# Ring slots staggered by 32 bytes, and matrix inputs placed at another offset for each pass

## The chip, the cores and the metric

The kernel runs on one core of one Trainium2 chip. The metric is device time in microseconds (us): the median of the runs. An execution has a span, from its first to its last recorded instruction, and a time that is a little longer.

## The reference, cut to what matters

Two transformer blocks of two layers each follow one another on 256 tokens of width 1024, all in float32. The first block mixes (latent attention, a short convolution, stick-breaking attention) and then sends each token to 16 of 16,384 experts in each of 8 heads. The second block has windowed attention with 256 context tokens, a Fourier mix, and a gated feed-forward pass of width 2816, for the latent tokens and, in its first layer, for the context too.

```
def token_block(args):                        # experts of the first block
    u = jnp.take(u_tab, eb, axis=0)
    act = jax.nn.gelu(jnp.einsum('tkd,td->tk', u, hb), approximate=False)
    vv = jnp.take(v_tab, eb, axis=0)
    return jnp.einsum('tk,tkd->td', gb * act, vv)
...
def swiglu(h, w_gate, w_up, w_down):          # feed-forward of the second block
    return (jax.nn.silu(h @ w_gate) * (h @ w_up)) @ w_down
```

## The kernel before, in words

Nothing is gathered for the experts: all 16,384 are computed for all 256 tokens, and a matrix of gates that is mostly zero is multiplied in between the two products. So each expert layer is two large dense products, with the tables U (up) and V (down) streamed once.

**A product in three parts.** A float32 product runs as three fast matmuls of the type fp32r: high times high, high times low, low times high (mm3, L293 to L296). A weight tile of 128 x 1024 comes by DMA into a slot of the ring raw (5 slots, issued by SP); for each half of 512 columns ACT writes the rounded high part wh (L261) and DVE the rest wl (L263). Helper wtile (L271) does this; wh and wl have 5 slots each. TensorE's reading sets a slot free for ACT.

**Two roles of the ring.** A matmul has a stationary operand of 128 x 128, loaded by LDWEIGHTS while the matmul ahead still runs, and a moving operand whose columns are then streamed.
- On the up side (gemm_t, L298) wh and wl are stationary, and the input (hh and hl, f or mix) is moving, 256 columns long. Groups pact (U), pwq (expert queries), pwg and pwu (gate and up), pw (input projection), and sq, sk, cb, cc, ch.
- On the down side wh and wl are moving, 512 columns long, and the activations are stationary: acc (V, with WHL), and po (with a and b, the feed-forward activations, or with mix). In both down sides the four outputs of a tile are taken in turn over tokens tb and halves n, three matmuls each, so that the moving slot changes every three matmuls. kw is a kept copy of such weights.

**Where the operands lie.** The addresses below are those in the built program, in bytes of a partition, modulo 256. "Distance" is the moving operand's address less the stationary one's, modulo 256, from -127 to 128. In the kernel before a slot is 2048 bytes long, so all slots of wh and wl lie at 192. hh, hl and f lie at 224 on the up side; WHL, a and b at 192 on the down side (pool tiles of SHIFT = 56 floats more give this); mixT and the second block's pw input at 224. Of the 15,624 split matmuls, 11,184 have 256 columns (10,608 at distance +32, 480 at +64, 96 at -64), 96 have 416 columns (-64), and 4344 have 512 columns (4104 at 0, 240 at -32; those are the first po stages on mix). The scores of the second block's attention, psc, are fp32r matmuls too, of 256 columns at distance 0; like the other small products of attention they are not in these counts.

**Order.** Each engine runs a list written out by the program; the tile scheduler orders it, and the sizes and offsets of tiles enter only through which tile shares memory with which.

Of the kernel before, what the change touches and what calls it, by code (L numbers as in the profile page):

```python
# [25 lines left out]
F32 = mybir.dt.float32  # L26
F32R = mybir.dt.float32r
# [9 lines left out]
S, D, L = 256, 1024, 2  # L37
KB = D // 128
# [3 lines left out]
FB = 22  # L42
# [163 lines left out]
def kernel(ctx: ExitStack, tc: tile.TileContext, a: dict, out: bass.AP):  # L206
    nc = tc.nc
    V, SC, T, G, SP = nc.vector, nc.scalar, nc.tensor, nc.gpsimd, nc.sync
# [3 lines left out]
    ring = ctx.enter_context(tc.tile_pool(name="ring", bufs=3))  # L212
    dram = ctx.enter_context(tc.tile_pool(name="dram", bufs=1, space=DRAM))
    RAW, NHL = 5, 5
# [39 lines left out]
    def raw_tile(src, shape):  # L254
        r = ring.tile([128] + shape, F32, name="raw", tag="raw", bufs=RAW)
        SP.dma_start(r, src)
        return r

    def split(dst_h, dst_l, src):
        with after(PIN.get("act")):  # L260
            SC.activation(dst_h, src, AF.Copy)  # L261
        with after(PIN.get("dve")):
            return V.tensor_tensor(dst_l, src, dst_h, op=OP.subtract).ins  # L263

    LAST = [None]
    PIN = {}

# [3 lines left out]
    def wtile(src, shape, cuts=None, keep=None):  # L271


        r = raw_tile(src, shape)
        parts = []
        c0 = 0
        for cut in cuts or [shape[0] // 2] * 2:
            sh = [cut] + shape[1:]
            h, lo = [(keep or ring).tile([128] + sh, F32R, name=nm, tag=nm, bufs=4 if keep else NHL) for nm in ("wh", "wl")]
            LAST[0] = split(h, lo, r[:, c0:c0 + cut])  # L280
            parts.append((h, lo))
            c0 += cut
        return parts
# [2 lines left out]

    SHIFT = 56

    def shifted(p, nm):
        t = p.tile([128, SHIFT + 2 * FB * S + 8], F32R, name=nm)[:, SHIFT:SHIFT + 2 * FB * S]  # L290
        return [t[:, i * FB * S:(i + 1) * FB * S].rearrange("p (f t) -> p f t", f=FB) for i in range(2)]

    def mm3(o, lh, ll, rh, rl, first, last):  # L293
# [518 lines left out]
    def peer(l, nxt):  # L812
# [2 lines left out]
        st.enter_context(banks(f"pa{l}", a=4, g=3))  # L815
        stpa = ExitStack()
        pa = stpa.enter_context(pool(f"peer{l}", side="right"))
        hh = pa.tile([128, KB, S], F32R, name="hh", tag="ha")
        hl = pa.tile([128, 2048 + SHIFT + 8], F32R, name="hl", tag="hb")[:, :2048].rearrange("p (k t) -> p k t", k=KB)
        idxT = pa.tile([128, 4, S], F32, name="idxT", tag="c")  # L820
        hot = pa.tile([128, 1 + 3 * NHOT, 128], F16, name="hot", tag="d")
        iota16 = hot[:, 0]
# [2 lines left out]
        with pool(f"topk{l}") as p:  # L825
            sh, sc = mod_cols(1, l, 3), mod_cols(1, l, 4)
# [16 lines left out]
            s = [p.tile([128, 16, 128], F32, name=f"s{tb}") for tb in range(2)]  # L843
# [160 lines left out]
        n = (128 - j) // 2  # L1004
# [6 lines left out]
        stb = ExitStack()  # L1011
        stb.enter_context(banks(f"pb{l}", acc=2, m=3))
        acc = [bank([128, 2, 512], f"acc{tb}", "acc") for tb in range(2)]
        Ws = pa.tile([128, 4, 2, S], F32, name="Ws", tag="ha")
        WHL = pa.tile([128, 2048 + SHIFT + 8], F32R, name="WHL", tag="hb")[:, SHIFT:SHIFT + 2048]
        WHL = WHL.rearrange("p (a b c t) -> p a b c t", a=2, b=2, c=2)
        stl, stk = ExitStack(), ExitStack()
        held = {}
# [6 lines left out]
        order = [120, 122, 124, 126] + list(range(0, 120, 2))  # L1025
# [45 lines left out]
        lgb = stl.enter_context(pool(f"lgb{l}", side="right")).tile([128, 2, D], F32, name="lgb")  # L1071
        for i in range(2):
            SP.dma_start(lgb[:, i], bcast_row(a["rows1"][l, 2 + i], D))
        rl = pa.tile([128, 2, D], F32, name="rl2", tag="ha")
        for tb in range(2):
            if l:
                next(nxt)
# [28 lines left out]
    def second_layer(l, p0, xc, c2, cosT, sinT, sm2, sink, pre):  # L1106
        both = l == 0
# [7 lines left out]
        def proj_out(p, s, src, nkt, mh, ml, gpart, row, tags=("mix", "gpr", "jk"), keep=None, jkp=None, mid=None,  # L1115
                     last=False):


            ssq = [p0.tile([128, 2], F32, name=f"sq{tb}", bufs=2) for tb in range(2)]
            gpr = p.tile([128, 2, D], F32, name="gpr", tag=tags[1])  # L1120
            gr, pr = gpr[:, 0], gpr[:, 1]
            SP.dma_start(pr, bcast_row(row, D))
            mod_row(gr, 2, l, gpart, s)
            V.tensor_tensor(gr, gr, pr, op=OP.mult)
            ps = [[bank([128, 512], "po", "m") for tb in range(2)] for n in range(2)]

            def mul(n, kt, tb, w):
                t = slice(128 * tb, 128 * tb + 128)
                for c in range(2):
                    k = 2 * kt + c  # L1130
                    mm3(ps[n][tb], mh[:, k, t], ml[:, k, t], w[c][0][:, 0], w[c][1][:, 0], k == 0, k == 2 * nkt - 1)

            def gated(n, tb):
                V.tensor_tensor(mixs[:, tb, n], ps[n][tb], gr[:, 512 * n:512 * n + 512], op=OP.mult)

            def square(n, tb):
                jk = (jkp or p).tile([128, 512], F32, name="jk", tag=tags[2], bufs=1)
                SC.activation(jk, ps[n][tb], AF.Square, accum_out=ssq[tb][:, n:n + 1])
                if n == 0:
                    gated(n, tb)  # L1140

            def tail(tb):
                ss = p0.tile([128, 1], F32, name="ss", bufs=2)
                V.tensor_tensor(ss, ssq[tb][:, 0:1], ssq[tb][:, 1:2], op=OP.add)
                r = rms_from(ss, D)
                gated(1, tb)
                x = xs[s][:, tb]
                if last:
                    for n in range(2):
                        c = slice(512 * n, 512 * n + 512)  # L1150
                        V.scalar_tensor_tensor(x[:, c], mixs[:, tb, n], r, x[:, c], op0=OP.mult, op1=OP.add)
                        SP.dma_start(out[0, 128 * tb:128 * tb + 128, c], x[:, c])
                else:
                    V.scalar_tensor_tensor(x, flat(mixs[:, tb]), r, x, op0=OP.mult, op1=OP.add)

            mixs = p.tile([128, 2, 2, 512], F32, name="mix", tag=tags[0])
            for n in range(2):
                ws = []
                for kt in range(nkt):
                    if keep and n:  # L1160
                        w = keep.tile([128, 2, 2, 512], F32R, name=f"kw{kt}")
                        r = raw_tile(src[n, kt], [2, 512])
                        for c in range(2):
                            split(w[:, c, 0], w[:, c, 1], r[:, c])
                        ws.append([(w[:, c, 0:1], w[:, c, 1:2]) for c in range(2)])
                        continue
                    w = wtile(src[n, kt], [2, 512])
                    if n and kt >= nkt - 2:
                        ws.append(w)
                    else:  # L1170
                        for tb in range(2):
                            mul(n, kt, tb, w)
                    if mid and (n, kt) == mid[0]:
                        mid[1]()
                for tb in range(2):
                    for kt, w in enumerate(ws, nkt - len(ws)):
                        mul(n, kt, tb, w)
                    square(n, tb)
                    if n:
                        tail(tb)  # L1180
# [250 lines left out]
        H, act, fp = {}, {}, {}  # L1431
# [4 lines left out]
        early = []  # L1436

        def tops(s, hp, px, ne=0):
            H[s] = [hp.tile([128, KB, S], F32R, name=f"f{i}{s}", tag=f"f{i}") for i in range(2)]
            cs = cols(l, s, 3, 8, "f")  # L1440
            for tb in range(2):
                hf = make_hT(px[tb], xs[s][:, tb], "rms", cs[0], cs[1], *H[s], 128 * tb, "m", px.count(px[tb]) if px[tb] is not fx else 1)
                for i in range(ne):
                    if tb == 0:
                        early.append((raw_tile((a["wg"], a["wu"])[i % 2][l, i // 2], [KB, 128]), bank([128, S], "pg", "m")))
                    gemm_early(early[i][1], early[i][0], hf, 128 * tb)
# [16 lines left out]


        fa1 = stp.enter_context(pool(f"ffa{l}"))
        act[order[0]] = shifted(fa1, "a")
        if both:
            fh0 = stp.enter_context(pool(f"ffg{l}"))
            sta = ExitStack()
# [3 lines left out]
        for s in order:  # L1473
            if both and s == 0:
                ex.run()
                stv.close()
                fa0 = sta.enter_context(pool(f"ffb{l}", side="right"))
                act[0] = shifted(fa0, "b")
            for f in range(FB):
                if s:  # L1480
                    ex.run(18.0 / (FB - 2))
                pgu = [e[1] for e in early[2 * f:2 * f + 2]] if s == 0 else []
                for nm in ("wg", "wu")[len(pgu):]:
                    pgu.append(bank([128, S], "p" + nm, "m"))
                    gemm_t(pgu[-1], wtile(a[nm][l, f], [KB, 128]), *H[s], 0, S)
                pg, pu = pgu
                sg = fx.tile([128, S], F32, name="sg", bufs=2)
                SC.activation(sg, pg, AF.Silu)
                V.tensor_tensor(sg, sg, pu, op=OP.mult)
                split(act[s][0][:, f], act[s][1][:, f], sg)  # L1490
                if s and f == FB - 6:
                    tops(0, fh0, [fx, fx])
# [46 lines left out]
```

## Time and profile before

| | us |
|---|---|
| median of 3 runs (lowest, highest) | 2849.2 (2847.5, 2852.63) |
| profiled execution: time, span | 2851.75, 2849.8 |
| TensorE matmul (PE) busy, share of the span | 2783.1, 98% |
| weight load (PEld) | 2437.5, 86% |
| VectorE (DVE) | 2197.0, 77% |
| ScalarE (ACT) | 1672.4, 59% |

The profiled execution lies inside the range of the runs. A matmul's record overlaps the next one's, since matmuls are pipelined; how long one occupies TensorE is read as the time from its start to the next one's start, and over a row of them as the difference of two starts divided by the intervals between. Mean durations of groups (280 to 390 ns) are not that time.

### The profile page before, as it was taken

How to read it: one execution, taken by the hardware profiler on the slowest of the kernel's cores; microseconds unless marked ns; L12 is line 12 of the kernel's file. 1: busy time of each engine (PE TensorE's matmuls, PEld its weight loads, DVE VectorE, ACT ScalarE, POOL GpSimd, SP SyncE). 2: the span in 40 equal slices, each digit the busy share in tenths (PEclk: the TensorE clock that was granted, in tenths of full speed). 3: DMA queues.
4: the chain of work that ended last, by engine and by line, in shares of the span. 5: the costliest groups of instructions: out<-in, count | busy, mean ns of one | idle time of the engine just before them, and what ended most of it. 6: DMA issues, size and time to landing. Idle time of an engine off the chain costs nothing.

```text
span 2849.8 us, 53010 instructions
## 1 busy us (share of the span) xinstructions
PE 2783.1 (98%) x19114; PEld 2437.5 (86%) x19114; DVE 2197.0 (77%) x5110; ACT 1672.4 (59%) x3459; POOL 39.2 (1%) x50
## 2 busy tenths in 40 slices
PE   7989999999999999999999999999999999998999
PEld 4569999998887766899999888878769999887997
DVE  4459999887789767799899777898769766577565
ACT  3435558885555445555799655555546555566554
POOL 0000000000000000000000000000000000000000
PEclk9999999999999999999999999999999999999999
DMA  9785775667789866576666777977647665652455
GB/s 325 234 275 180 241 233 193 200 202 253 240 275 310 302 240 236 200 236 230 208 198 198 238 240 241 335 270 221 225 157 268 215 204 189 205 184 70 159 187 162
DMA packets 188114, 639.76 MB, mean 224 GB/s; under 512 B 22709, under 2 KB 24117, under 8 KB 187209
## 3 DMA queue, kind: packets, MB, share of 16 engines
q1 hardware_dynamic: 179208, 604.90, 64.4%
q10 hardware_dynamic: 8640, 31.46, 2.8%
q8 instruction: 150, 2.46, 0.3%
q14 instruction: 116, 0.94, 0.1%
HBM read 600.06 MB, written 34.64 MB: 223 GB/s over the span
## 4 chain that ended last, share of the span: by engine, by line
PE 90%; DVE 4%; DMA 3%; ACT 2%; issue 1%; POOL 0%; SPq 0%; DVEq 0%; POOLq 0%; ACTq 0%
PE pact L294 9%; PE pact L296 8%; PE pact L295 8%; PE acc L295 8%; PE acc L296 8%; PE acc L294 8%; PE po L294 3%; PE po L295 3%; PE po L296 3%; PE adap L348 2%; DMA adaw<-in_ada_dram 2%; PE pwu L296 2%; PE pwu L294 2%; PE pwu L295 2%; PE pwg L294 2%; PE pwg L296 2%
## 5 line engine op out<-in xcount | busy, mean ns | idle before, releaser
L261 ACT ACTIVATE wh<-raw 128x512 fp32r<-128x512 f32 (+1 forms) x1636 | 1008.4, 627 | 809.0 <-PE acc L296 272.8
L263 DVE TENSOR_TENSOR wl<-raw,wh 128x512 fp32r<-128x512 f32 (+1 forms) x1636 | 1089.8, 683 | 378.1 <-ACT wh L261 372.8
L294 PE MATMUL pact<-hh,wh 128*128 128x256 f32 x2048 | 583.6, 285 | 0.0
L296 PE MATMUL pact<-hh,wl 128*128 128x256 f32 x2048 | 572.5, 280 | 0.2 <-DVE wl L263 0.2
L295 PE MATMUL pact<-hl,wh 128*128 128x256 f32 x2048 | 571.4, 279 | 0.0
L295 PE MATMUL acc<-wl,WHL 128*128 128x512 f32 x1024 | 399.3, 390 | 1.6 <-DVE wl L263 1.6
L294 PE MATMUL acc<-wh,WHL 128*128 128x512 f32 x1024 | 397.9, 390 | 1.2 <-ACT WHL L261 1.2
L296 PE MATMUL acc<-wh,WHL 128*128 128x512 f32 x1024 | 398.7, 389 | 0.0
L295 PEld LDWEIGHTS pact<-hl,wh 128*128 128x128 f32 x2048 | 385.5, 188 | 0.0
L294 PEld LDWEIGHTS pact<-hh,wh 128*128 128x128 f32 x2048 | 385.3, 188 | 0.0
L296 PEld LDWEIGHTS pact<-hh,wl 128*128 128x128 f32 x2048 | 384.9, 188 | 0.4 <-DVE wl L263 0.4
L295 PEld LDWEIGHTS acc<-wl,WHL 128*128 128x128 f32 x1024 | 192.2, 188 | 44.2 <-DVE wl L263 3.8
L294 PEld LDWEIGHTS acc<-wh,WHL 128*128 128x128 f32 x1024 | 192.2, 188 | 43.9 <-ACT WHL L261 3.3
L296 PEld LDWEIGHTS acc<-wh,WHL 128*128 128x128 f32 x1024 | 192.2, 188 | 40.4 <-DVE WHL L263 0.9
L993 ACT ACTIVATE hot<-hot,idxT 128x128 f16<-128x128 f16 x512 | 174.0, 402 | 1.3 <-DVE hot L992 1.2
L992 DVE TENSOR_SCALAR hot<-hot,idxT 128x128 f16<-128x128 f16 x512 | 158.0, 309 | 20.1 <-PE pG L994 19.8
L296 PE MATMUL pwu<-f,wl 128*128 128x256 f32 x512 | 143.1, 279 | 1.6 <-DVE wl L263 1.6
L294 PE MATMUL pwg<-f,wh 128*128 128x256 f32 x512 | 143.1, 280 | 0.0
L296 PE MATMUL pwg<-f,wl 128*128 128x256 f32 x512 | 143.0, 279 | 0.0
L295 PE MATMUL pwg<-f,wh 128*128 128x256 f32 x512 | 142.9, 279 | 0.0
L294 PE MATMUL pwu<-f,wh 128*128 128x256 f32 x512 | 142.8, 279 | 0.0
L295 PE MATMUL pwu<-f,wh 128*128 128x256 f32 x512 | 142.8, 279 | 0.0
(475 smaller groups left out, 5075.4 us busy)
## 6 DMA issues: line engine op xcount, KB each, us to landing
raw<-in_U_dram SPq DMA_DIRECT2D x256, 512.0 KB, 3.6
raw<-in_V_dram SPq DMA_DIRECT2D x256, 512.0 KB, 4.2
adaw<-in_ada_dram SPq DMA_DIRECT2D x192, 512.0 KB, 6.1
raw<-in_wg_dram SPq DMA_DIRECT2D x66, 512.0 KB, 4.2
raw<-in_wu_dram SPq DMA_DIRECT2D x66, 512.0 KB, 3.4
raw<-in_wd_dram SPq DMA_DIRECT2D x66, 512.0 KB, 4.2
spill<-gab ACTq DMA_DIRECT2D x60, 512.0 KB, 5.1
Ws<-spill SPq DMA_DIRECT2D x120, 256.0 KB, 3.8
```

Source lines behind the costliest of these rows:

```text
L261: SC.activation(dst_h, src, AF.Copy)
L263: return V.tensor_tensor(dst_l, src, dst_h, op=OP.subtract).ins
L294: T.matmul(o, lh, rh, start=first, stop=False)
L295: T.matmul(o, lh, rl, start=False, stop=False)
L296: T.matmul(o, ll, rh, start=False, stop=last)
L348: T.matmul(ps[32 * q:32 * q + 32, :], cvec(blk, k), r[h][:, 512 * (q % 2):512 * (q % 2) + 512], start=k == 0, stop=k == KB - 1, skip_group ...
L992: V.tensor_scalar(B, iota16, i2, g, op0=OP.is_equal, op1=OP.mult)
L993: SC.activation(B2, B, AF.Copy, scale=share)
```

## The change

The ring's wh and wl tiles become 516 floats wide, of which 512 are used, so that slots lie 2080 bytes apart, 32 bytes on from one to the next modulo 256. A first dummy load of 128 x 672 into raw and a gap tile of 24 floats, which is set to zero once, set the order and place of the ring's tags. The inputs are put at other offsets by placed and shifted. The pools' tiles grow by 64 floats to allow it, and the kernel's entry takes a smaller scratch area for DMA descriptors. No matmul is added, dropped or reshaped.

| operand, modulo 256 | before | after |
|---|---|---|
| wh and wl, slots 1 to 5 | 192 each | 192, 224, 0, 32, 64 |
| hh, hl of the mixer's projection; catH, wok | 0; 0, 0 | 160; 160, 160 |
| hh, hl of the experts, layer 0 / 1 | 224 / 224 | 224 / 48 |
| WHL, layer 0 / 1 | 192 / 192 | 192 / 112 |
| f: context; latent layer 0; latent layer 1 | 224 each | 128; 112; 176 |
| a; b | 192; 192 | 192; 208 |
| mixT and the first layer's pw input; kw | 224; 224 | 128; 224 |

Distances of the split matmuls after the change, in counts:

| distance | -112 | -96 | -80 | -64 | -48 | -32 | -16 | 0 |
|---|---|---|---|---|---|---|---|---|
| 256 columns | 408 | 1164 | 408 | 1128 | 192 | 816 | 876 | 720 |
| 512 columns | 312 | 72 | 306 | 48 | 306 | 0 | 54 | 594 |

| distance | 16 | 32 | 48 | 64 | 80 | 96 | 112 | 128 |
|---|---|---|---|---|---|---|---|---|
| 256 columns | 684 | 744 | 888 | 336 | 876 | 444 | 1068 | 432 |
| 512 columns | 54 | 414 | 54 | 468 | 360 | 498 | 354 | 450 |

```diff
--- before.py
+++ after.py
@@ -262,6 +262,17 @@
         with after(PIN.get("dve")):
             return V.tensor_tensor(dst_l, src, dst_h, op=OP.subtract).ins
 
+
+    def part_tile(p, sh, nm, bufs):
+        n = math.prod(sh)
+        t = p.tile([128, 516], F32R, name=nm, tag=nm, bufs=bufs)[:, :n] if p is ring else p.tile([128, n], F32R, name=nm, tag=nm, bufs=bufs)
+        return t if len(sh) == 1 else t.rearrange("p (a b) -> p a b", a=sh[0])
+
+    raw_tile(a["w1n"][0, 0:128, :], [672])
+    part_tile(ring, [4], "wh", NHL)
+    V.memset(ring.tile([128, 24], F32, name="gap", bufs=1), 0.0)
+    part_tile(ring, [4], "wl", NHL)
+
     LAST = [None]
     PIN = {}
 
@@ -276,7 +287,7 @@
         c0 = 0
         for cut in cuts or [shape[0] // 2] * 2:
             sh = [cut] + shape[1:]
-            h, lo = [(keep or ring).tile([128] + sh, F32R, name=nm, tag=nm, bufs=4 if keep else NHL) for nm in ("wh", "wl")]
+            h, lo = [part_tile(keep or ring, sh, nm, 4 if keep else NHL) for nm in ("wh", "wl")]
             LAST[0] = split(h, lo, r[:, c0:c0 + cut])
             parts.append((h, lo))
             c0 += cut
@@ -286,8 +297,12 @@
 
     SHIFT = 56
 
-    def shifted(p, nm):
-        t = p.tile([128, SHIFT + 2 * FB * S + 8], F32R, name=nm)[:, SHIFT:SHIFT + 2 * FB * S]
+    def placed(p, nm, tag, at):
+
+        return p.tile([128, 2048 + 64], F32R, name=nm, tag=tag)[:, at:at + 2048].rearrange("p (k t) -> p k t", k=KB)
+
+    def shifted(p, nm, at):
+        t = p.tile([128, 2 * FB * S + 64], F32R, name=nm)[:, at:at + 2 * FB * S]
         return [t[:, i * FB * S:(i + 1) * FB * S].rearrange("p (f t) -> p f t", f=FB) for i in range(2)]
 
     def mm3(o, lh, ll, rh, rl, first, last):
@@ -815,8 +830,7 @@
         st.enter_context(banks(f"pa{l}", a=4, g=3))
         stpa = ExitStack()
         pa = stpa.enter_context(pool(f"peer{l}", side="right"))
-        hh = pa.tile([128, KB, S], F32R, name="hh", tag="ha")
-        hl = pa.tile([128, 2048 + SHIFT + 8], F32R, name="hl", tag="hb")[:, :2048].rearrange("p (k t) -> p k t", k=KB)
+        hh, hl = [placed(pa, nm, tag, 20 * l) for nm, tag in (("hh", "ha"), ("hl", "hb"))]
         idxT = pa.tile([128, 4, S], F32, name="idxT", tag="c")
         hot = pa.tile([128, 1 + 3 * NHOT, 128], F16, name="hot", tag="d")
         iota16 = hot[:, 0]
@@ -1011,8 +1025,8 @@
         stb = ExitStack()
         stb.enter_context(banks(f"pb{l}", acc=2, m=3))
         acc = [bank([128, 2, 512], f"acc{tb}", "acc") for tb in range(2)]
-        Ws = pa.tile([128, 4, 2, S], F32, name="Ws", tag="ha")
-        WHL = pa.tile([128, 2048 + SHIFT + 8], F32R, name="WHL", tag="hb")[:, SHIFT:SHIFT + 2048]
+        Ws = pa.tile([128, 2048 + 64], F32, name="Ws", tag="ha")[:, :2048].rearrange("p (a b t) -> p a b t", a=4, b=2)
+        WHL = placed(pa, "WHL", "hb", SHIFT - 20 * l).rearrange("p k t -> p (k t)")
         WHL = WHL.rearrange("p (a b c t) -> p a b c t", a=2, b=2, c=2)
         stl, stk = ExitStack(), ExitStack()
         held = {}
@@ -1071,7 +1085,7 @@
         lgb = stl.enter_context(pool(f"lgb{l}", side="right")).tile([128, 2, D], F32, name="lgb")
         for i in range(2):
             SP.dma_start(lgb[:, i], bcast_row(a["rows1"][l, 2 + i], D))
-        rl = pa.tile([128, 2, D], F32, name="rl2", tag="ha")
+        rl = pa.tile([128, 2048 + 64], F32, name="rl2", tag="ha")[:, :2048].rearrange("p (a d) -> p a d", a=2)
         for tb in range(2):
             if l:
                 next(nxt)
@@ -1117,7 +1131,7 @@
 
 
             ssq = [p0.tile([128, 2], F32, name=f"sq{tb}", bufs=2) for tb in range(2)]
-            gpr = p.tile([128, 2, D], F32, name="gpr", tag=tags[1])
+            gpr = p.tile([128, 2048 + 64], F32, name="gpr", tag=tags[1])[:, :2048].rearrange("p (a d) -> p a d", a=2)
             gr, pr = gpr[:, 0], gpr[:, 1]
             SP.dma_start(pr, bcast_row(row, D))
             mod_row(gr, 2, l, gpart, s)
@@ -1153,7 +1167,7 @@
                 else:
                     V.scalar_tensor_tensor(x, flat(mixs[:, tb]), r, x, op0=OP.mult, op1=OP.add)
 
-            mixs = p.tile([128, 2, 2, 512], F32, name="mix", tag=tags[0])
+            mixs = p.tile([128, 2048 + 64], F32, name="mix", tag=tags[0])[:, :2048].rearrange("p (a n d) -> p a n d", a=2, n=2)
             for n in range(2):
                 ws = []
                 for kt in range(nkt):
@@ -1436,7 +1450,7 @@
         early = []
 
         def tops(s, hp, px, ne=0):
-            H[s] = [hp.tile([128, KB, S], F32R, name=f"f{i}{s}", tag=f"f{i}") for i in range(2)]
+            H[s] = [placed(hp, f"f{i}{s}", f"f{i}", 52 if not both else 60 - 20 * s) for i in range(2)]
             cs = cols(l, s, 3, 8, "f")
             for tb in range(2):
                 hf = make_hT(px[tb], xs[s][:, tb], "rms", cs[0], cs[1], *H[s], 128 * tb, "m", px.count(px[tb]) if px[tb] is not fx else 1)
@@ -1463,7 +1477,7 @@
 
 
         fa1 = stp.enter_context(pool(f"ffa{l}"))
-        act[order[0]] = shifted(fa1, "a")
+        act[order[0]] = shifted(fa1, "a", 16)
         if both:
             fh0 = stp.enter_context(pool(f"ffg{l}"))
             sta = ExitStack()
@@ -1475,7 +1489,7 @@
                 ex.run()
                 stv.close()
                 fa0 = sta.enter_context(pool(f"ffb{l}", side="right"))
-                act[0] = shifted(fa0, "b")
+                act[0] = shifted(fa0, "b", 60)
             for f in range(FB):
                 if s:
                     ex.run(18.0 / (FB - 2))
@@ -1532,7 +1546,7 @@
     from concourse.bass_utils import run_bass_kernel_spmd
 
     arrays = _layout(inputs)
-    nc = bacc.Bacc("TRN2", target_bir_lowering=False, num_devices=1)
+    nc = bacc.Bacc("TRN2", target_bir_lowering=False, num_devices=1, dynamic_dma_scratch_size=1024)
     build(nc, arrays)
     r = run_bass_kernel_spmd(nc, [{f"in_{n}_dram": v for n, v in arrays.items()}], core_ids=[0])
     return r.results[0]["out_0_dram"]
```

On SP, at the program's start, this stands before and then after the change (names as in the tables; adaw are the weights of the modulation, x the tokens):

```order
1 L235 DMA k_69<-in_k1c_dram 128x519
2 L307 DMA c_73<-in_c_dram 128x8
3 L308 DMA c_73<-in_c_dram 128x16
4 L519 DMA pi<-in_pos_dram 128x256
5 L336 DMA adaw<-in_ada_dram 128x1024 x6
```

```order
1 L235 DMA k_69<-in_k1c_dram 128x519
2 L256 DMA raw<-in_w1n_dram 128x672
3 L322 DMA c_79<-in_c_dram 128x8
4 L323 DMA c_79<-in_c_dram 128x16
5 L534 DMA pi<-in_pos_dram 128x256
6 L351 DMA adaw<-in_ada_dram 128x1024 x6
```

The dummy load stands ahead of c, pi and adaw; nothing else moved there. On TensorE, at the entry of the second layer's experts (hTp are transpositions of the normalised tokens, pwq the query products, pss the key scores), first before and then after:

```order
7014 L501 MATMUL hTp<-k_69,xn 128x128 x3
7015 L479 MATMUL pwq<-hf,raw 128x128 x6
...
7023 L479 MATMUL pwq<-hf,raw 128x128 x5
7024 L501 MATMUL hTp<-k_69,xn 128x128 x4
7025 L479 MATMUL pwq<-hf,raw 128x128 x24
7026 L929 MATMUL pss_13463<-pk,pqT 128x128
```

```order
7014 L516 MATMUL hTp<-k_69,xn 128x128 x2
7015 L494 MATMUL pwq<-hf,raw 128x128 x6
...
7023 L494 MATMUL pwq<-hf,raw 128x128 x5
7024 L516 MATMUL hTp<-k_69,xn 128x128 x5
7025 L494 MATMUL pwq<-hf,raw 128x128 x24
7026 L943 MATMUL pss_13469<-pk,pqT 128x128
```

One transposition moved from the first group to the last. On DVE, at the same place (hf are the transposed tokens, hl their low part), before and then after:

```order
1676 L507 TENSOR_SCALAR hf<-hTp,mcols 128x128
1677 L263 TENSOR_TENSOR hl<-hf,hh 128x4x128
1678 L507 TENSOR_SCALAR hf<-hTp,mcols 128x128
1679 L263 TENSOR_TENSOR hl<-hf,hh 128x4x128
1680 L263 TENSOR_TENSOR wl<-raw,wh 128x512 x2
1681 L263 TENSOR_TENSOR hl<-hf,hh 128x4x128
1682 L263 TENSOR_TENSOR wl<-raw,wh 128x512 x2
1683 L507 TENSOR_SCALAR hf<-hTp,mcols 128x128 x2
1684 L263 TENSOR_TENSOR hl<-hf,hh 128x4x128
1685 L359 TENSOR_TENSOR abias<-adap,abias 128x512
```

```order
1677 L263 TENSOR_TENSOR hl<-hf,hh 128x4x128
1678 L263 TENSOR_TENSOR wl<-raw,wh 128x512
1679 L263 TENSOR_TENSOR hl<-hf,hh 128x4x128
1680 L263 TENSOR_TENSOR wl<-raw,wh 128x512 x3
1681 L522 TENSOR_SCALAR hf<-hTp,mcols 128x128 x4
1682 L263 TENSOR_TENSOR hl<-hf,hh 128x4x128 x2
1683 L374 TENSOR_TENSOR abias<-adap,abias 128x512
```

The same four hl stand there, and the last two now follow four hf in a row. Elsewhere the five engines issue the same instructions in the same order, but for a cast of constants (hot) that stands earlier on DVE and one pwq product behind a pair of pss instead of ahead of it.

## Rows read from the trace of the kernel before

**Rows 1.** The page: busy time, chain that ended last.

```profile
PE 2783.1 (98%) x19114; PEld 2437.5 (86%) x19114; DVE 2197.0 (77%) x5110; ACT 1672.4 (59%) x3459; POOL 39.2 (1%) x50
...
PE 90%; DVE 4%; DMA 3%; ACT 2%; issue 1%; POOL 0%; SPq 0%; DVEq 0%; POOLq 0%; ACTq 0%
```

**Rows 2.** Stretches: length, busy PE, PEld, DVE, ACT, POOL, clock, DMA share, GB/s.

```profile
250.00:640.00 390.00, 389.83 (x3556) 386.51 (x3555) 358.20 (x1135) 293.05 (x678) 0.00 (x0) 1.00 0.66 214
640.00:1035.00 395.00, 389.23 (x1773) 311.99 (x1772) 312.60 (x462) 205.24 (x357) 3.97 (x4) 1.00 0.81 273
```

**Rows 3.** Costliest groups: busy time, mean ns of one, idle time before, releaser.

```profile
L261 ACT ACTIVATE wh<-raw 128x512 fp32r<-128x512 f32 (+1 forms) x1636 | 1008.4, 627 | 809.0 <-PE acc L296 272.8
L263 DVE TENSOR_TENSOR wl<-raw,wh 128x512 fp32r<-128x512 f32 (+1 forms) x1636 | 1089.8, 683 | 378.1 <-ACT wh L261 372.8
```

**Rows 4.** What PE waited for: total us, times, longest.

```profile
PE adap L348 <- DMA adaw<-in_ada_dram: 23.8, 11, 8.3
PE psc L1361 <- ACT P L1379: 5.6, 4, 2.9
```

**Rows 5.** Timeline of PE, po on mix, distance -32: start, us.

```profile
2629.49 0.39 PE L295 MATMUL po<-wl,mix 128*128 128x512 f32 x1
...
2638.82 0.40 PE L296 MATMUL po<-wh,mix 128*128 128x512 f32 x1
```

**Rows 6.** Timeline of PE, po on kw, distance 0, right behind.

```profile
2639.05 0.40 PE L294 MATMUL po<-kw,mix 128*128 128x512 f32 x1
...
2649.71 0.39 PE L296 MATMUL po<-kw,mix 128*128 128x512 f32 x1
```

**Rows 7.** Timeline of PE, acc (distance 0) behind a stop.

```profile
895.75 0.50 PE L295 MATMUL acc<-wl,WHL 128*128 128x512 f32 x1 [0.41 <-DVE wl L263]
896.09 0.39 PE L296 MATMUL acc<-wh,WHL 128*128 128x512 f32 x1
...
897.25 0.39 PE L295 MATMUL acc<-wl,WHL 128*128 128x512 f32 x1
```

**Rows 8.** Timeline of PE, pact, distance +32.

```profile
599.95 0.28 PE L294 MATMUL pact<-hh,wh 128*128 128x256 f32 x1
...
601.60 0.28 PE L296 MATMUL pact<-hh,wl 128*128 128x256 f32 x1
```

**Rows 9.** Timeline of PE, sq, distance +64.

```profile
54.30 0.28 PE L294 MATMUL sq<-hh,wh 128*128 128x256 f32 x1
...
57.01 0.28 PE L296 MATMUL sq<-hh,wl 128*128 128x256 f32 x1
```

**Rows 10.** Timeline of PE, pn, distance -64.

```profile
49.41 0.28 PE L294 MATMUL pn<-wh,hh 128*128 128x256 f32 x1
...
49.76 0.35 PE L294 MATMUL pn<-wh,hh 128*128 128x416 f32 x1
...
50.31 0.28 PE L294 MATMUL pn<-wh,hh 128*128 128x256 f32 x1
```

**Rows 11.** Timeline of PE, psc, distance 0.

```profile
2035.85 0.28 PE L1362 MATMUL psc<-k,qS 128*128 128x256 f32 x1
...
2036.56 0.28 PE L1362 MATMUL psc<-k,qS 128*128 128x256 f32 x1
```

**Rows 12.** Timeline of SP's queue at the start; and the page's GB/s by slice.

```profile
1.18 0.42 SPq L307 DMA_DIRECT2D c<-in_c_dram  x1
1.64 0.42 SPq L308 DMA_DIRECT2D c<-in_c_dram  x1
...
GB/s 325 234 275 180 241 233 193 200 202 253 240 275 310 302 240 236 200 236 230 208 198 198 238 240 241 335 270 221 225 157 268 215 204 189 205 184 70 159 187 162
```

**Rows 13.** Timeline of DVE, then PE, at the second expert layer's entry.

```profile
1160.96 0.69 DVE L263 TENSOR_TENSOR hl<-hf,hh 128x512 fp32r<-128x512 f32 x1 [1.19 <-ACT hh L261]
...
1163.77 1.06 PE L929 MATMUL pss<-pk,pqT 128*128 128x128 f32 x8
1164.58 0.36 PE L294 MATMUL pwq<-hh,wh 128*128 128x256 f32 x1
```

## The prediction

> **What bounds the kernel now.** I read the page's busy times and chain first. TensorE is busy for 98% of the span, and 90% of the chain that ended last runs through it [rows 1]. By stretches it is closer still: 389.83 of 390 us in an up side of the experts, 389.23 of 395 us in a down side, both at a granted clock of 1.00, the upper level of 2.4 GHz [rows 2]. The costliest groups then tell which way the ring waits. ACT's wh waited 272.8 us for acc to free a slot, its largest single wait, and DVE's wl waited for wh; so the ring is full and TensorE empties it [rows 3]. TensorE's own waits are small: 23.8 us in all for modulation weights, 5.6 us for the next one [rows 4]. What counts is therefore the time that one matmul takes while nothing waits, start to next start. That is read from the timeline of PE.
>
> The change alters only where operands lie, so I sorted the matmuls by the distance of moving from stationary operand and by column count, and read a row of intervals for each distance that occurs.
> - 512 columns: at -32, 40 intervals from 2629.49 to 2638.82, 233.3 ns each [rows 5]. At 0, in the same stage a moment later, 47 intervals from 2639.05 to 2649.71, 226.8 ns [rows 6]. The difference is 6.5 ns, with the same engines at work around it. After a stop at distance 0 the first five intervals, 896.09 to 897.25, take 232 ns [rows 7], and then it settles at 227.
> - 256 columns: at +32, 14 intervals from 599.95 to 601.60, 117.9 ns [rows 8]; at +64, 23 from 54.30 to 57.01, 117.8 [rows 9]; at -64, 3 from 49.41 to 49.76, 116.7 [rows 10]; at 0, 6 from 2035.85 to 2036.56, 118.3 [rows 11].
> At 2.4 GHz the columns alone would take 106.7 and 213.3 ns. So 10 to 12 ns of a 256-column matmul, and 13 to 20 ns of a 512-column one, are something else; the distance moves at least 6.5 ns of it on 512 columns, and no more than 1.6 ns on 256 columns in the four distances that the kernel shows.
>
> **The change part by part.** Sums are against the profiled execution (2851.75 us), which lies 2.55 us above the median of 2849.2; the sum carries over to the median.
>
> 1. 256 columns at -32 (816) and -16 (876). No row of before has these with 256 columns. Bounds: 0, since the four distances shown lie together, and 6.5 ns, the 512-column price of -32, which is 1692 x 6.5 = 11.0 us. I take half the price at -32 (816 x 3.3 = 2.7) and a quarter at -16, which lies half-way to 0 (876 x 1.6 = 1.4): +4.1 us.
>
> 2. 256 columns at 0 (720) and 16 (684). At 0 the row shows 118.3 against 117.9, +0.4; half of that at 16. 720 x 0.4 + 684 x 0.2 = +0.4 us, between 0 and 1404 x 1.6 = 2.2.
>
> 3. 256 columns at 48 or more either way: 7344 matmuls. The nearest rows are +64 and -64: -0.1 and -1.2 ns against +32, the latter from 3 intervals read to 0.01 us. I take 0; by -64 alone it would be -8.8 us, and by the row at 0 +2.9. The 744 that stay at +32 change nothing.
>
> 4. 512 columns. 240 leave -32: 240 x -6.5 = -1.6 us. The 4104 at distance 0 lose one common distance; 192 of them (pm) keep it. In the others the ring's slot, and with it the distance, changes every three matmuls, fewer than the five that a stopped row at distance 0 took to settle [rows 7]. That is 3912 matmuls. Bounds: 0, if a change of slot without a stop disturbs nothing and the new distances (none is -32, 54 are -16) settle like 0; and 232 - 226.8 = 5.2 ns on each, 20.3 us, if they never settle. A stop lets both streams start anew and a change of slot does not, so I stay nearer the low end, a quarter: +5.1 us.
>
> 5. The start. The dummy load stands ahead of c, pi and adaw on SP, and TensorE's first work waits for adaw [rows 4]. One issue is 1.64 - 1.18 = 0.46 us; its 344 KB at the first slice's 325 GB/s are 1.06 us [rows 12]. Between the two, +0.8 us, since nothing covers it. The memset of gap is 24 columns on an idle DVE: 0.
>
> 6. The moved transposition at the second layer's experts. The last hl ended at 1161.65 and TensorE came to the product after pss at 1164.58 [rows 13]: 2.9 us of room. Behind the change the last two hl, 0.69 us each, follow four hf; that fits under the pq products and key scores that hide it. 0, and at most +1 us if the room is gone.
>
> 7. ACT and DVE write and read at the new slot addresses. wh took 627 and wl 683 ns on average, at the old addresses alone [rows 3]. If that grew, DVE would be late first: it is busy 358.2 of 390 us in the up side [rows 2], so wl would have to grow by about 9% before TensorE waited. I take 0 here; the cover is the ring's five slots.
>
> The sum is 4.1 + 0.4 + 0 - 1.6 + 5.1 + 0.8 + 0 = +8.8 us. On the profiled execution that makes 2860.6, on the median 2858.0 us. With every term at its low end it is -8.8 - 1.6 + 0.5 = -9.9; at its high end 11.0 + 2.2 + 2.9 - 1.6 + 20.3 + 1.1 + 1.0 = +36.9. So the forecast's own range is 2839 to 2886.
>
> **The rivals.**
>
> Faster: the surplus over the columns is paid when the next weights are read near the place that the moving operand is being read, and far distances pay less. The place is the up sides: 7344 matmuls of 256 columns at 48 or more, and 3228 of 512 columns. For it: the surplus is there, 10 ns and more on each of 15,624 matmuls, and two places in one stage differ by 6.5 ns [rows 5, 6]. Against it: +64 and -64 are far already, and their rows are within 1.2 ns of +32 [rows 8 to 10]. If the far ones lost half of the 6.5 ns step, that is 7344 x 3.3 + 3228 x 3.3 = -34.9; term 4's +5.1 falls away, and 4.1 + 0.4 - 1.6 + 0.8 stay: -31.2, or 2818 us. It decides from (8.8 + 5.7) / 10,572 = 1.4 ns for each far matmul.
>
> No change: what the rows show at -32 is particular to that stage, or settles whatever the slot. Then only the start is left: 2850.0 us. For it: 256 columns hardly tell distances apart. Against it: rows 5 and 6 differ by 3% with the same shapes and the same engines at work. The Trainium skill speaks for this rival: "SBUF — State Buffer", section "Who interferes with whom", says that PE waits on nobody, and "TensorE: Matmul & The Clock Gate", section "Step-by-step: what each phase is for", that moving and stationary operand have a read port each, so that loading the next weights takes nothing from the running matmul. By that rule distances would be worth nothing and the sum would be the start alone; the trace does not agree, since 233.3 against 226.8 ns is a difference in place only.
>
> Much slower: no 512-column row settles (20.3) and -32 and -16 cost the full step on 256 columns (11.0): with the start and the gain on mix, +30.5, or 2880 us. For it: five slots in five relations, new every three matmuls. Against it: the stop of rows 7 is a harder break.
>
> That ACT or DVE becomes the bound I leave out: it needs the 9% of term 7.
>
> **How the numbers follow.** A measurement of this kernel can tell about 0.2%, 5.7 us, from no change. Forecast 0.38, faster 0.33, no change 0.19, much slower 0.10. Of the forecast's own range a part near its low end is within 5.7 us of before, and a small part below. That gives slower 0.43, same 0.23, faster 0.34. The predicted time is 2858 us. The range that should hold it 8 times in 10 reaches from the faster rival's figure, 2818, to 2883, between the much slower rival and the sum of all high ends; the likeliest case's own is 2839 to 2886.
>
> **What would show it.** Right: starts of 256-column matmuls at -32 and -16 some ns further apart than at +64, others within 1.5 ns of before; acc and po at 227 to 229 ns and no more exactly repeating; adap's first wait up by under a microsecond; TensorE still at 99% of the expert stretches. Wrong: pact, pwg and pwu below 115 ns on the far slots (the faster rival), acc at 232 (much slower), or TensorE waiting for wl in the up side, which would mean that slot addresses matter to DVE and that term 7 was mis-sized.

## The result, and the profile after

The changed kernel takes 2877.2 us (median of 4 runs, 2873.4 to 2881.3) against 2848.6 us for the kernel before on the same chip: a ratio of 1.0098, 95% interval 1.0086 to 1.0111, or 28.6 us slower. The forecast was 2858 us, slower by 9; its range held the time, and the time lies by the rival that was called much slower (2880).

The page of the changed kernel shows the same picture as before [rows 1, 3]: TensorE is busy 98%, wh and wl take as long as they did (627 and 684 ns), and DVE waits no less. The granted clock is 1.00 in both expert stretches, as before [rows 2].

```profile
PE 2814.2 (98%) x19114; PEld 2448.5 (85%) x19114; DVE 2203.3 (77%) x5111; ACT 1674.8 (58%) x3459; POOL 40.3 (1%) x50
...
L261 ACT ACTIVATE wh<-raw 128x512 fp32r<-128x512 f32 (+1 forms) x1636 | 1010.4, 627 | 835.7 <-PE acc L311 284.0
L263 DVE TENSOR_TENSOR wl<-raw,wh 128x512 fp32r<-128x512 f32 (+1 forms) x1636 | 1093.5, 684 | 397.9 <-ACT wh L261 392.0
...
L310 PE MATMUL acc<-wl,WHL 128*128 128x512 f32 x1024 | 404.0, 395 | 0.0
```

The matmuls themselves take longer from start to start. The timeline of PE in acc shows ten intervals of 233 ns where one of before settled at 227 [rows 6, 7]; the distances in this stretch are 0, 128, 96 and 64, three matmuls each.

```profile
947.73 0.40 PE L310 MATMUL acc<-wl,WHL 128*128 128x512 f32 x1
...
950.06 0.40 PE L311 MATMUL acc<-wh,WHL 128*128 128x512 f32 x1
```

In pact one can watch the slots pass, the timeline of PE again: 7 intervals from 600.78 at distance 0 take 120.0 ns each; 10 from 602.49 at 32 take 117; 10 from 603.78 at -96 take 119. Before, all were at 32 and took 117.9 in the stretch of [rows 8], and 117.2 on average over both layers.

```profile
600.78 0.28 PE L309 MATMUL pact<-hh,wh 128*128 128x256 f32 x1
...
601.62 0.28 PE L310 MATMUL pact<-hl,wh 128*128 128x256 f32 x1
...
602.49 0.28 PE L310 MATMUL pact<-hl,wh 128*128 128x256 f32 x1
...
603.66 0.28 PE L311 MATMUL pact<-hh,wl 128*128 128x256 f32 x1
603.78 0.28 PE L309 MATMUL pact<-hh,wh 128*128 128x256 f32 x1
...
604.97 0.28 PE L310 MATMUL pact<-hl,wh 128*128 128x256 f32 x1
```

I took the start-to-start times of all split matmuls from both traces, left out those beside a stop, and multiplied each group's difference of means by its count in the trace. This is as large as the whole loss:

| group | count | before, ns | after, ns | us |
|---|---|---|---|---|
| acc | 3039 | 226.80 | 232.11 | +16.1 |
| po | 1064 | 228.27 | 232.25 | +4.2 |
| pact | 5867 | 117.17 | 117.89 | +4.2 |
| pwg and pwu | 3062 | 116.67 | 118.26 | +4.9 |
| all others | 2056 | | | +1.3 |
| sum | | | | +30.7 |

The spans differ by 29.3 us (2879.1 against 2849.8). With the start, 1.4 us, the table comes to 32.1, which is 2.8 us too much. The matmuls beside a stop, which the table leaves out, took less than before: counted with them, acc grew by 13.3 us and not by 16.1. At the start TensorE's first work moved from 8.34 to 9.71 us:

```profile
9.71 1.07 PE L363 MATMUL adap<-adaw,c 128*32 128x512 f32 x2 [9.71 <-DMA adaw<-in_ada_dram]
```

### The profile page after: what moved, and what is told of

Its sections match the earlier page's. It is cut to its first block, busy times and chain, and to the rows that moved or that the text cites. A ratio compares the mean times of both kernels' runs of the same rounds, so it can differ in the third digit from the quotient of the medians.

```text
span 2879.1 us, 53009 instructions
## 1 busy us (share of the span) xinstructions
PE 2814.2 (98%) x19114; PEld 2448.5 (85%) x19114; DVE 2203.3 (77%) x5111; ACT 1674.8 (58%) x3459; POOL 40.3 (1%) x50
## 4 chain that ended last, share of the span: by engine, by line
PE 91%; DVE 3%; DMA 3%; ACT 2%; issue 1%; POOL 0%; SPq 0%; DVEq 0%; POOLq 0%; ACTq 0%
PE pact L309 9%; PE pact L311 8%; PE pact L310 8%; PE acc L309 8%; PE acc L311 8%; PE acc L310 8%; PE adap L363 3%; PE po L311 3%; PE po L309 3%; PE po L310 3%; DMA adaw<-in_ada_dram 2%; PE pwu L311 2%; PE pwu L309 2%; PE pwg L309 2%; PE pwg L311 2%; PE pwu L310 2%
## 5 line engine op out<-in xcount | busy, mean ns | idle before, releaser
L309 PE MATMUL acc<-wh,WHL 128*128 128x512 f32 x1024 | 402.6, 394 | 1.2 <-ACT WHL L261 1.2
L311 PE MATMUL acc<-wh,WHL 128*128 128x512 f32 x1024 | 403.8, 394 | 0.0
```

What stands on the lines that cost most here:

```text
L309: T.matmul(o, lh, rh, start=first, stop=False)
L311: T.matmul(o, ll, rh, start=False, stop=last)
```

## The experiments

Two theories stood against each other. One, settling: a row of 512-column matmuls settles as long as its distance stays, and each change of slot starts it anew (the forecast's term 4). The other, distances: each distance has its own time, wherever slots change. In the first four expectations "theory" is settling; from the run with the stagger alone on, "theory" is that of distances.

**Distances by themselves.** A kernel of nothing but matmuls of the two shapes, in the kernels' order of three. In down a slot is the moving operand, in up the stationary one. The arguments are a name, the ring (flat has all slots at one place modulo 256, step 32 bytes on from one to the next), the offset of the other operand in floats, the matmuls to a slot, and the number of threes.

```
for i in range(16):
    down("d" + "abcdefghijklmnop"[i], flat, 4 * i, 3, 32)
for i in range(16):
    up("u" + "abcdefghijklmnop"[i], flat, 4 * i, 12, 32)
for nm, every in (("dx", 3), ("dy", 6), ("dz", 12), ("dw", 24)):
    down(nm, step, 0, every, 40)
for nm, every in (("ux", 12), ("uy", 48)):
    up(nm, step, 8, every, 80)
```

> This kernel leaves the whole computation out and issues only matmuls of the two shapes, in the kernels' order of three, with constant data: 96 of 512 columns at each of 16 distances with one slot place (groups da to dp: 0, -16, -32 ... -112, 128, 112 ... 16), 96 of 256 columns at each (ua to up: 0, 16, 32 ... 112, 128, -112 ... -16), then slots 32 bytes on from one to the next, changed every 3, 6, 12 and 24 matmuls (dx, dy, dz, dw; distances 0 to 128) and, for 256 columns, every 12 and 48 (ux, uy; distances 32 to -96). Theory (a row of 512 columns settles while its distance stays, and every change of slot starts it anew): da, at one distance, 227 ns after its first matmuls, dc 233, the others each a constant of its own; dx 231 to 233, and dy, dz, dw fall step by step towards the mean of their distances at rest. Rival (each distance has its own time, settled or not): dx, dy, dz and dw agree within 1 ns, and each is the mean of da, do, dm, dk, di. For 256 columns the theory expects ux and uy alike within 0.5 ns and each distance between 115 and 120.

It ran once, at a granted clock of 1.00. The first matmul of a group and that of the next one enclose 96 intervals. Timeline of PE: da (distance 0) 21.77 us or 226.8 ns each, dc (-32) 22.39 us or 233.2; ua (0) 11.52 us or 120.0, uh (112) 10.88 us or 113.3.

```profile
24.89 0.39 PE L251 MATMUL da<-flat,act 128*128 128x512 f32 x1
46.66 0.39 PE L251 MATMUL db<-flat,act 128*128 128x512 f32 x1
...
68.42 0.39 PE L251 MATMUL dc<-flat,act 128*128 128x512 f32 x1
90.81 0.40 PE L251 MATMUL dd<-flat,act 128*128 128x512 f32 x1
...
380.57 0.28 PE L265 MATMUL ua<-act,flat 128*128 128x256 f32 x1
392.09 0.28 PE L265 MATMUL ub<-act,flat 128*128 128x256 f32 x1
...
460.39 0.28 PE L265 MATMUL uh<-act,flat 128*128 128x256 f32 x1
471.27 0.28 PE L265 MATMUL ui<-act,flat 128*128 128x256 f32 x1
```

Means of the last 40 intervals of each group, in ns:

| distance | -112 | -96 | -80 | -64 | -48 | -32 | -16 | 0 |
|---|---|---|---|---|---|---|---|---|
| 512 columns | 233.3 | 234.3 | 232.0 | 233.4 | 233.3 | 233.4 | 226.7 | 226.7 |
| 256 columns | 118.7 | 117.3 | 119.3 | 113.4 | 119.2 | 118.3 | 117.2 | 120.0 |

| distance | 16 | 32 | 48 | 64 | 80 | 96 | 112 | 128 |
|---|---|---|---|---|---|---|---|---|
| 512 columns | 226.7 | 233.3 | 233.4 | 228.8 | 230.0 | 233.3 | 233.3 | 233.3 |
| 256 columns | 118.7 | 116.7 | 118.3 | 117.8 | 120.0 | 120.1 | 113.3 | 118.7 |

Distance 0 was thus one of three low places for 512 columns among sixteen, not the usual case. On 256 columns 112 and -64 lie below the 115 that was expected as the least. For the changing slots dx, dy, dz and dw took 232.8, 232.1, 231.8 and 231.5 ns; their five distances at rest average 231.1. For dx and dw, 120 intervals each, the rows are:

```profile
561.71 0.39 PE L251 MATMUL dx<-step,act 128*128 128x512 f32 x1
...
589.65 0.39 PE L251 MATMUL dy<-step,act 128*128 128x512 f32 x1
...
645.31 0.39 PE L251 MATMUL dw<-step,act 128*128 128x512 f32 x1
...
673.09 0.28 PE L265 MATMUL ux<-act,step 128*128 128x256 f32 x1
```

Most of the loss is there however rarely the slot changes; its change adds 1.7 ns at three matmuls a slot and 0.4 at 24. In dw the first three at distance 0 took 231 to 232 ns and all later ones 227, so the settling that the forecast spoke of exists, but little hangs on it. ux and uy agree (117.9 and 118.0), so on 256 columns it does not matter how often the slot changes. Both lie 0.9 ns above the mean of their five distances at rest (117.1), and one distance makes that up: at -64, which alone took 113.4, uy stays at 117.9 for all its 48 matmuls (46 intervals below).

```profile
718.53 0.28 PE L266 MATMUL uy<-act,step 128*128 128x256 f32 x1
...
723.95 0.28 PE L267 MATMUL uy<-act,step 128*128 128x256 f32 x1
```

Settling held for distance 0, the rival for the size.

**The ring with one slot place, inputs at the new offsets.** Against the changed kernel:

```diff
-        t = p.tile([128, 516], F32R, name=nm, tag=nm, bufs=bufs)[:, :n] if p is ring else ...
+        t = p.tile([128, 512], F32R, name=nm, tag=nm, bufs=bufs)[:, :n] if p is ring else ...
...
-    V.memset(ring.tile([128, 24], F32, name="gap", bufs=1), 0.0)
+    V.memset(ring.tile([128, 64], F32, name="gap", bufs=1), 0.0)
```

> The kernel after, with the ring's slots 2048 bytes apart again, so that each pass has one distance throughout, while the passes keep their new offsets (acc at 0 in layer 0 and at 80 in layer 1, a at -96, b at -16; pact at 32 and 112; pwg and pwu at -64, -16 and 16). Theory (settling): acc and po near 227 ns in every pass but where a distance settles high as -32 does, 2847 to 2856 us in all. Rival (distances): by the means that the kernel after shows for each distance, acc in layer 1 at 231, a at 234, b at 232, so +6.4, +3.9 and +1.5 us, less about 3 us for pact at 112: 2858 us. If neither slots nor distances matter but the new tiles' layout does, 2877.

2850.7 us, ratio to before 1.0008 (0.9999 to 1.0018). So with the stagger undone the loss is gone, but not because distances stopped to matter: acc at 80 in the second layer took 230.0 ns (the distance alone: 230.0), a at -96 234.2 (234.3), and pact at 112 in the second layer 114.5 on average (113.3); in a stretch where no other product stands between, it took 113.6. The losses and gains cancel: acc +4.9, po +5.5, pact -8.6 and pwq -0.5 us, +1.6 with the rest. The time lay in the theory's bounds by that accident; the groups are the rival's. One row fits neither: b at -16 took 233.2 ns, 44 intervals from 2414.45 to 2424.71 in the timeline, against 226.7 for that distance alone.

```profile
1240.09 0.28 PE L310 MATMUL pact<-hl,wh 128*128 128x256 f32 x1
...
1242.59 0.28 PE L311 MATMUL pact<-hh,wl 128*128 128x256 f32 x1
...
2414.45 0.39 PE L309 MATMUL po<-wh,b 128*128 128x512 f32 x1
...
2424.71 0.40 PE L311 MATMUL po<-wh,b 128*128 128x512 f32 x1
```

(The pact rows: 22 intervals, 113.6 ns.)

**Six matmuls to a slot instead of three.** The changed kernel, with the down side's loops over n and tb exchanged.

```diff
                 for n in range(2):
-                    mm3(acc[tb][:, n], WH[:, c, t], WL[:, c, t], *v[c][n], ...)
+                    for tb in tbs:
+                        t = slice(128 * tb, 128 * tb + 128)
+                        mm3(acc[tb][:, n], WH[:, c, t], WL[:, c, t], *v[c][n], ...)
```

> The kernel after, with the two loops of the expert down side exchanged, so that a slot serves six matmuls in a row instead of three. Theory (each change of slot costs the rows that follow it): the 5.3 ns that acc gained over before falls to about half, 3072 x 2.6 = 8 us: 2869 us. Rival (distances): the same distances are met as often, 2877 us and acc still at 232 ns.

2876.9 us, ratio to before 1.0102 (1.0085 to 1.0119), against 1.0098 for the changed kernel, and acc at 232.0 ns where that had 232.1. Half as many changes of slot saved nothing. In the timeline of PE, 17 intervals of acc take 232.4 ns each:

```profile
946.66 0.40 PE L309 MATMUL acc<-wh,WHL 128*128 128x512 f32 x1
...
950.61 0.39 PE L311 MATMUL acc<-wh,WHL 128*128 128x512 f32 x1
```

**The dummy load alone.** The kernel before with one line, `raw_tile(a["w1n"][0, 0:128, :], [672])`, ahead of LAST.

> The kernel before with the dummy load of 128 x 672 added at the start and nothing else. Both theories: 0.5 to 1.5 us more than before, all of it in the first wait for adaw, so 2850; acc stays at 227 ns, pact at 117.

2852.7 us, ratio 1.0009 (0.9997 to 1.0020): no difference that can be told, and acc at 226.8 and pact at 117.2 ns. In the trace TensorE's first work begins 0.70 us later than before, 9.04 against 8.34:

```profile
9.04 1.92 PE L349 MATMUL adap<-adaw,c 128*32 128x512 f32 x4 [9.04 <-DMA adaw<-in_ada_dram]
```

**The stagger alone for the experts.** The changed kernel with `20 * l` made 0 and `SHIFT - 20 * l` made SHIFT.

> The kernel after, with the experts' inputs (hh, hl, WHL) of both layers where layer 0 has them, which is their old place; the ring's slots stay 32 bytes apart, and the feed-forward inputs stay as in the kernel after. Theory (the slots of the ring alone spread the distances, and most distances are dearer than the two of before): no better than the kernel after, 2872 to 2882 us, acc 231 to 233 ns, pact near 118. Rival (the offset of the second layer's experts is the harm): half of pact's and acc's loss comes back, 2867 us.

2882.1 us, ratio 1.0118 (1.0103 to 1.0134), acc 232.3 and pact 118.2 ns. With one slot place nothing clear of noise was lost (1.0008 above), so the stagger does the harm; the second layer's own offset gave some 2 us back by groups (in the changed kernel acc lost 16.1 us and pact 4.2, here 16.8 and 5.8).

**One slot place, and every big pass at its cheap distance.** Against the ring with one slot place (the second kernel has 40 for both 20s):

```diff
-        hh, hl = [placed(pa, nm, tag, 20 * l) for nm, tag in (("hh", "ha"), ("hl", "hb"))]
+        hh, hl = [placed(pa, nm, tag, 20) for nm, tag in (("hh", "ha"), ("hl", "hb"))]
...
-        WHL = placed(pa, "WHL", "hb", SHIFT - 20 * l).rearrange("p k t -> p (k t)")
+        WHL = placed(pa, "WHL", "hb", SHIFT).rearrange("p k t -> p (k t)")
...
-            H[s] = [placed(hp, f"f{i}{s}", f"f{i}", 52 if not both else 60 - 20 * s) for i in range(2)]
+            H[s] = [placed(hp, f"f{i}{s}", f"f{i}", 20) for i in range(2)]
...
-        act[order[0]] = shifted(fa1, "a", 16)
+        act[order[0]] = shifted(fa1, "a", SHIFT)
...
-                act[0] = shifted(fa0, "b", 60)
+                act[0] = shifted(fa0, "b", SHIFT)
```

> One slot place for the whole ring, as in one_place, with every big pass at the distance that was cheapest by itself: 112 for pact, pwq, pwg and pwu (113.3 ns alone against 116.7 at 32), 0 for acc and po of a and b (226.7). Theory (each distance has its own time): 6768 matmuls of the experts from 117.1 to 114.5, as in the second layer of one_place, and 3072 of the feed-forward pass from 116.7 to 114: 26 us less than before, 2820 to 2827 us. Rival (the gain in one_place's second layer came with something else in that layer): 2845 to 2850.

> As all_112, with -64 in place of 112 (113.4 ns alone): theory 2820 to 2829 us, rival 2845 to 2850.

2827.1 us at 112 (ratio 0.9924, 0.9911 to 0.9938) and 2821.7 us at -64 (0.9908, 0.9893 to 0.9924). Both are faster than the kernel before and the changed kernel. pact went to 114.5 and 114.0 ns, pwg and pwu to 113.4, acc stayed at 226.8; by groups that is -26.5 and -29.3 us. The page and the timeline of the one at -64: 19 intervals from 2199.80 to 2201.95, 113.2 ns.

```profile
PE 2755.0 (98%) x19114; PEld 2409.3 (85%) x19114; DVE 2192.6 (78%) x5111; ACT 1666.9 (59%) x3459; POOL 39.1 (1%) x50
```

```profile
2199.80 0.28 PE L310 MATMUL pwu<-f,wh 128*128 128x256 f32 x1
...
2201.95 0.28 PE L311 MATMUL pwg<-f,wl 128*128 128x256 f32 x1
```

**The dear distances.** The same with offsets 56 for hh, hl and f, and 64 for WHL, a and b.

> One slot place for the whole ring, as in all_112, with the big passes at the distances that were dear by themselves: 0 for pact, pwq, pwg and pwu (120.0 ns alone), -32 for acc and po of a and b (233.3 alone). Theory (the distance that a pass keeps sets its time, both ways): 9840 matmuls of 256 columns at 119.5 to 120 against 117.0, +25 to +30 us, and 3864 of 512 columns at 233.3 against 226.8, +25 us: 2898 to 2905 us. Rival (a ring with one slot place is at rest and near the old time, and the harm of the change was the changing of slots): 2849 to 2865 us.

2901.9 us, ratio 1.0166 (1.0143 to 1.0189), 51.5 us between the medians: the theory's number, with one slot place and all other work as before. pact took 119.7, pwg and pwu 120.0, acc 233.3 ns (timeline of acc: 9 intervals in 2.10 us):

```profile
944.62 0.40 PE L310 MATMUL acc<-wl,WHL 128*128 128x512 f32 x1
...
946.72 0.40 PE L310 MATMUL acc<-wl,WHL 128*128 128x512 f32 x1
```

**How a distance is entered.** A second kernel of matmuls alone, for the row at -16 that fitted neither theory: 24 matmuls at another distance, or a stop, ahead of 72 at the one measured.

```
for h, pre in (("z", 0), ("t", -32)):
    down("pre", flat, AT[pre], 3, 8)
    down("d" + h + NM[d], flat, AT[d], 3, 24)
pause()
down("ds" + NM[d], flat, AT[d], 3, 24)
```

> Only matmuls with constant data again; the rest of the computation is left out. 72 of 512 columns at distances 0, -16, 16, -32, 80, 64, 112 behind 24 at 0 (dz), behind 24 at -32 (dt) and behind a stop of some us (ds); 96 of 256 columns at 112, -64, 32, 0 (uz, ut, us) likewise; then 0 and -16 at four places of the moving operand, 64 bytes apart (ea to eg, fa to fg). Theory (a distance has one time to which every row settles): dz, dt and ds end alike, 226.7 at 0 and 16, 233.3 at -32 and 112. But b at -16 took 233.3 ns in one_place and 226.7 in bench, so at -16 at least the rival (what a row settles to depends on how it was entered) should show: 226.7 in dz and 233.3 in dt or ds. If neither differs there, the place itself counts, and fa to fg differ.

The rival showed, in the one execution of this kernel, at a granted clock of 1.00. At -16, behind 0 (dzb) 71 intervals took 16.09 us, 226.6 ns each; behind -32 (dtb) 16.56 us, 233.2:

```profile
90.59 0.39 PE L251 MATMUL dzb<-flat,act 128*128 128x512 f32 x1
...
106.68 0.40 PE L253 MATMUL dzb<-flat,act 128*128 128x512 f32 x1
...
112.52 0.40 PE L251 MATMUL dtb<-flat,act 128*128 128x512 f32 x1
...
129.08 0.40 PE L253 MATMUL dtb<-flat,act 128*128 128x512 f32 x1
```

Behind the stop it ended at 233.4. The same two levels showed at 112 (226.7 behind 0, 233.3 behind -32 or a stop), and at 16 (226.7 against 228.3). At 0 every entry ended at 226.7, at -32 every one at 233.3, at 64 at 228.9 and at 80 at 230.0. On 256 columns 112 and -64 came to 113.3 from each of the three entries tried here, though uy above stayed high at -64; 0 came to 120.0, and 32 ended at 117.8 or 116.7. The place of the moving operand by itself made no difference: 226.7 at four places for distance 0, and for -16 entered from it.

## Why the prediction was right in sign and short in size

- **What bounds the kernel** held: TensorE at 98%, ACT and DVE unmoved, the loss in start-to-start times but for the start's 1.4 us.
- **Term 4, the 512-column matmuls** (forecast +5.1, and -1.6 for mix) is the term of the sum that was mis-sized. It measured +20.4 us with mix, above the high end of its bounds, which with mix is 18.7. The gain on mix itself was 0.2 us and not 1.6 (233.2 to 232.5 ns), since the distances that it moved to are dear too. The reason behind the quarter, that new distances settle like 0 unless disturbed, was wrong: at rest, entered one from the next as in the first kernel of matmuls, the ten distances of acc average 231.7 ns, 5 ns above 0, so by this estimate 4.9 of the 5.3 ns would be there with no change of slot at all. The two distances that the trace showed were the low and nearly the highest level, and I had treated the low one as usual.
- **Terms 1 to 3, the 256-column matmuls** (+4.5) measured +10 us, and in other places. In the changed kernel -32 took 118.2 and -16 117.2 against 117.0 at 32: 1.2 us, not 4.1. At 0 it was 119.5 where the row of psc had 118.3 [rows 11]. The far distances, put at 0 because +64 and -64 looked like +32, cost 7.9 us (at 80, 119.6; at 96, 120.0; at -96, 118.6), beyond the bound of 2.9. The prediction also read one level as the time of +32: 117.9 [rows 8] is the upper of two that the kernel before shows at that distance. pact ran at 116.7 from some 260 to 430 us (21 intervals below) and at 117.8 from 1230 to 1370, and pwg and pwu at 116.7 throughout, so the 1.2 ns that -64 seemed to gain [rows 10] is none against the lower level.

```profile
300.04 0.28 PE L294 MATMUL pact<-hh,wh 128*128 128x256 f32 x1
...
302.49 0.28 PE L294 MATMUL pact<-hh,wh 128*128 128x256 f32 x1
```

- **Term 5, the start**: TensorE's first work came 1.37 us later, against 0.8, and 0.70 with the dummy load alone. What added the rest in the changed kernel was not tried.
- **Terms 6 and 7** held. The last hl ends at 1171.00 (DVE's timeline), and TensorE comes to the product at 1173.55: 2.6 us of room [rows 13].

```profile
1170.31 0.69 DVE L263 TENSOR_TENSOR hl<-hf,hh 128x512 fp32r<-128x512 f32 x1 [0.32 <-ACT hh L261]
...
1173.55 0.36 PE L309 MATMUL pwq<-hh,wh 128*128 128x256 f32 x1
```

- **The rivals.** The much slower one had the size right (2880), in part by luck. Its 20.3 us on 512 columns were met, but by distances that are dear at rest and not by rows that never settle. Its 11.0 us for -32 and -16 on 256 columns were 1.2, and 7.9 from the far distances stood in their place. The faster one was right that some far distances cost less: two, 112 and -64, bring 256 columns to 113.3 ns. Its "half a step for all far distances" was wrong, since most of them are dearer, and a staggered ring cannot hold one distance. No change is ruled out by 2821.7 against 2901.9 us for the same instructions at other places. That PE waits on nobody (the Trainium skill, "SBUF — State Buffer", section "Who interferes with whom") is said of the engines among each other; the kernels of matmuls alone show the dear and the cheap distances with the other engines next to idle (DVE 6 of 700 us, ACT 0 in the first of them), so what fails is the step from that rule to distances being worth nothing.

What stays open: what in the chip makes the levels. Most steady rows lie between 113.3 and 120.0 ns on 256 columns and between 226.7 and 233.3 on 512, a span of 6.7 ns for both; I did not find out what the steps are. That distances repeat after 256 bytes was taken for granted in sorting them and was not tested, and nothing finer than 16 bytes was. Nor was it tried whether a ring of slots can be laid out so that each change enters the low level.

## What to carry to other kernels

Where TensorE is the bound and weights are loaded for every matmul, look at start-to-start times by the distance of the two operands modulo 256, and measure every distance once by itself: here the cheapest and the dearest choice tried for the same instructions lie 80 us apart by their medians (on two chips, whose runs of the kernel before differ by 2 us), and 2.6% by their ratios to before. Then look at it in the kernel too, since a row can settle at another level there (b at -16). Keep one distance through a pass; the stagger spread each pass over five. A row or two that agree (here +64, -64 and +32) say nothing of the distances that the trace does not show.

## What the runs showed that was not expected

A row of matmuls can have two steady states at one and the same distance, and keep the one it entered: 226.7 or 233.3 ns at -16 and at 112 on 512 columns. 256 columns have such levels as well. In the kernel at -64, pact ran at 117.8 ns from some 270 to 340 us and from 350 us on at 113.3, with no change of distance (22 intervals each).

```profile
299.72 0.28 PE L310 MATMUL pact<-hl,wh 128*128 128x256 f32 x1
...
302.31 0.28 PE L311 MATMUL pact<-hh,wl 128*128 128x256 f32 x1
...
399.81 0.28 PE L310 MATMUL pact<-hl,wh 128*128 128x256 f32 x1
...
402.30 0.28 PE L311 MATMUL pact<-hh,wl 128*128 128x256 f32 x1
```

The Trainium skill, "TensorE: Matmul & The Clock Gate", section "Wait — 56ns, not 53.3ns?", has start-to-start at the columns' time at 2.4 GHz plus about 2.5 ns, which is an estimate of 109.2 and 215.8 ns for these two shapes. Here nothing came that near: the lowest steady rows of this order of three were 113.3 and 226.7 ns.
